# Four GpSimd subtractions of 256 columns for each weight tile's low half, in place of one of 1024

## The chip, the cores and the metric

The kernel runs on one core of a Trainium2 chip. Its time is the device time of one launch in microseconds (us). Of the kernel before there are three runs: 1603.31, 1604.33 and 1604.15 us, median 1604.15 us. A profile of one further execution gives the rows that are read here.

## What is computed

Two layers of a decoder trunk on an input of 512 positions by 1024 channels, float32. Each layer, shortened:

```python
h = rms_norm(x, attn_norm[i])
proj = h @ w_in[i]                      # 1024 x 5376: q, k, v of mixers A, B, C and three gates
ya = moba_attention(...)                # A: blocks of 256, causal
yb = sliding_window_sink_attention(...) # B: window 128, grouped queries, sinks
yc = differential_attention(...)        # C: softmax 1 - lam * softmax 2, then a norm
g = jax.nn.sigmoid(gates)
x = x + (g0 * (ya @ w_pa) + g1 * (yb @ w_pb) + g2 * (yc @ w_pc)) @ w_out[i]
h = rms_norm(x, mlp_norm[i])
u = causal_depthwise_conv(h @ w_up[i], conv_w[i], conv_b[i])
x = x + (silu(gate_u) * val_u) @ w_down[i]
```

## The kernel before

Every product with a weight matrix is computed from two halves of each operand. A weight tile (128 partitions by 1024 columns, `raw`) comes from memory by a transfer on SyncE's queue. ScalarE rounds it to a shorter format (`whi`), and the difference `raw - whi` is the low half (`wlo`). The activations have two halves in the same way (`h0..`, `h1..`, both shown as `h`; those of later products lie in buffers called `slot`). A product is three matmuls into PSUM (`d`): high by high, high by low, low by high. There are 248 weight tiles.

`w_prep` (line 634) makes the two halves of a tile. Line 643 ff. decide which engine subtracts: GpSimd (POOL in the profile) while attention threads are alive and its planned clock is not more than `POOL_LEAD` = 3 us past TensorE's, VectorE (DVE) otherwise. `pump` calls it up to three or four tiles ahead of TensorE; there are 4 buffers each for `whi` and `wlo` and 2 for `raw`, so the transfer of the next tile but one waits until the subtraction has read `raw`.

The order of all instructions is fixed while the program is built. `dense()` emits the weight products block by block. Attention (scores `s`, transposes and products with values `tp`, softmax on ScalarE and VectorE) runs as further threads, and the loop at the end of `trunk` lets a thread emit its next step when a table of planned clocks says that its engine and inputs are ready. That table is `Estimate`: each emitted instruction goes through `Clocked` (line 157; its call in line 168 is why all rows of the profile say L168), and `Estimate.cost` adds its planned duration to the engine's clock, for GpSimd `0.1 + 2.16e-3 * columns` (us). The planned clocks decide the order alone; on the chip the instructions wait for semaphores.

In softmax VectorE runs short chains for each head: the row maximum of the masked scores (`s<-s,mfull`, `mx`), its scaled negative (`nb`), after ScalarE's exponential the reciprocal (`rec`, for mixer C times lambda: `rl`), and scaled probabilities (`slot<-slot,rec`). Rotary embedding is made of products and sums of buffers (`temp`, `slot`). Scores and transposes lie in PSUM, the others in SBUF. GpSimd also computes powers (`rr`, `rsub`, `rn`) and small products (`slot<-slot,vecs`).

Of the kernel before, what the change touches and what calls it, by code (L numbers as in the profile page):

```python
# [11 lines left out]
F32 = mybir.dt.float32  # L12
# [142 lines left out]


class Clocked:
    """Runs an engine's instructions and keeps an estimate of when each one ends."""

    def __init__(self, est, eng, key):  # L160
        self._est, self._eng, self._key = est, eng, key
# [164 lines left out]
def trunk(ctx: ExitStack, tc: tile.TileContext, out: bass.AP, a: dict):  # L326
# [169 lines left out]
    def first_part(t, j):  # L496
        sl = slice(t * 128, (t + 1) * 128)
        ps = tps.get()
        for c in range(4):
            nc.tensor.transpose(ps[:, c, :], X[t][:, (4 * j + c) * 128:(4 * j + c + 1) * 128], identf)  # L500
        for c in range(4):
            k = 4 * j + c
            nc.scalar.activation(H[0, k][:, sl], ps[:, c, :], AF.Copy, scale=gain(0, k))
        for c in range(0, 4, 2):
            nc.scalar.copy(XT[2 * j + c // 2].rearrange("p (e t) -> p e t", e=2)[:, :, sl], ps[:, c:c + 2, :])
        for c in range(4):
            k = 4 * j + c
            nc.vector.scalar_tensor_tensor(H[1, k][:, sl], ps[:, c, :], gain(0, k), H[0, k][:, sl].bitcast(F32),
                                           op0=OP.mult, op1=OP.subtract)
        tps.put(ps)  # L510
# [123 lines left out]
    def w_prep(j):  # L634
        hi = est.alloc("whi", NW, wpool.tile([128, 1024], F32R, tag="whi", name="whi"))
        lo = est.alloc("wlo", NW, wpool.tile([128, 1024], F32R, tag="wlo", name="wlo"))
        raw = RAW.pop(j)
        nc.scalar.copy(hi, raw)
        if state["busy"]:
            t = est.ready(hi)  # L640
            pool = max(est.clock["POOL"], t) <= max(est.clock["DVE"], t) + POOL_BIAS
        else:
            pool = threads[1:] and est.clock["POOL"] <= est.clock["PE"] + POOL_LEAD
        if pool:
            nc.gpsimd.tensor_sub(lo, raw, hi.bitcast(F32))
        else:
            nc.vector.tensor_sub(lo, raw, hi.bitcast(F32))
        if j in wide:
            slots.put(raw)
        if j < 2:  # L650
            first_part(0, j)
        W[j] = (hi, lo)

    def pump(lead):
        while state["prep"] < min(state["fin"] + NW, lead, len(wt)):
            while state["dma"] < min(state["prep"] + ahead(), len(wt)):
                w_dma(state["dma"])
                state["dma"] += 1
            w_prep(state["prep"])
            state["prep"] += 1  # L660
        while state["dma"] < min(state["prep"] + ahead(), len(wt)):
            w_dma(state["dma"])
            state["dma"] += 1
# [888 lines left out]
    def eng_clock(eng):  # L1552
        if eng == "ANY":
            return min(est.clock["ACT"], est.clock["DVE"])
        return est.clock[eng]
# [6 lines left out]
    while threads:  # L1562
# [24 lines left out]
        for r, th in others:  # L1587
            c = eng_clock(th.cur[0])
# [62 lines left out]
```

## Time and profile before

| | |
|---|---|
| median of three runs | 1604.15 us (1603.31 to 1604.33) |
| span of the profiled execution (first to last instruction) | 1599.4 us |
| what the median has beside such a span | 4.75 us |
| TensorE busy | 1546.0 us (97%) |
| VectorE busy | 1077.5 us (67%) |
| ScalarE busy | 789.8 us (49%) |
| GpSimd busy | 293.6 us (18%), 175.5 us of it in 72 subtractions |

The page gives the span of the profiled execution and not its whole device time, so the span stands beside the median here. Shares are means over the whole program: attention of the first layer lies at about 55 to 365 us, that of the second at about 812 to 1160 us; around them are long stretches of weight products alone. The end of a matmul is modelled in the profile: the next one starts 0.23 us after one of 512 columns whose row says 0.39 us, so gaps of TensorE are shown too short by some 0.16 us each.

### The profile page before, as it was taken

The page shows a single profiled execution, that of the slowest core. Times are in us where ns is not written, and L with a number is a line of the kernel's source. Part 1 is how long each engine was busy: PE and PEld are TensorE (multiplying, and loading weights), DVE is VectorE, ACT ScalarE, POOL GpSimd, SP SyncE. Part 2 cuts the span into 40 slices and gives each one's busy share as a digit, 9 for nine tenths or more (in the row PEclk, how much of TensorE's full clock was granted, in tenths as well). Part 3 has the DMA queues.
Part 4 walks back from the last instruction along what each step waited for, and adds up shares of the span by engine and source line. Part 5 has one row for each costly group of instructions (what it writes and reads, how often), then busy time and mean ns, then how long its engine had stood idle before and what let it go on. Part 6 is the DMA issues. An engine that isn't in the chain of part 4 may idle for free.

```text
span 1599.4 us, 21003 instructions
## 1 busy us (share of the span) xinstructions
PE 1546.0 (97%) x7584; PEld 1283.9 (80%) x7584; DVE 1077.5 (67%) x2242; ACT 789.8 (49%) x1534; POOL 293.6 (18%) x243
## 2 busy tenths in 40 slices
PE   8999999999999999999998999999999999999999
PEld 6777787778878888888887887878788788888887
DVE  5998888988576655543269898797875856665321
ACT  7565656755344444333155666647634544443220
POOL 3443343321010000000044553323200100000000
PEclk9999999999999999999999999999999999999999
DMA  5423152223233233333332224322242233223331
GB/s 176 150 57 90 54 198 67 68 65 132 86 100 100 86 105 106 106 99 125 92 113 66 80 67 158 93 80 64 69 151 87 79 106 93 89 83 106 118 119 53
DMA packets 115495, 157.21 MB, mean 98 GB/s; under 512 B 18880, under 2 KB 71104, under 8 KB 115392
## 3 DMA queue, kind: packets, MB, share of 16 engines
q1 hardware_dynamic: 102768, 153.19, 30.6%
q10 hardware_dynamic: 12624, 2.69, 0.8%
q8 instruction: 60, 0.98, 0.2%
q14 instruction: 43, 0.35, 0.1%
HBM read 144.84 MB, written 11.01 MB: 97 GB/s over the span
## 4 chain that ended last, share of the span: by engine, by line
PE 73%; DVE 20%; ACT 3%; issue 2%; POOL 1%; DMA 0%; ACTq 0%; SPq 0%; DVEq 0%; POOLq 0%
PE d L168 67%; DVE slot L168 8%; PE tp L168 5%; DVE temp L168 4%; DVE s L168 2%; ACT slot L168 2%; DVE nb L168 2%; PE s L168 1%; DVE rl L168 1%; DVE wlo L168 1%; DVE h L168 1%; POOL rr L168 1%; ACT whi L168 1%; ACT temp L168 0%; DMA raw<-in_w_in 0%
## 5 line engine op out<-in xcount | busy, mean ns | idle before, releaser
L168 PE MATMUL d<-h,whi 128*128 128x512 f32 x2176 | 683.0, 395 | 8.6 <-DVE h L168 4.5
L168 PEld LDWEIGHTS d<-h,whi 128*128 128x128 f32 x2176 | 399.9, 189 | 88.5 <-DVE h L168 5.6
L168 PE MATMUL d<-h,wlo 128*128 128x512 f32 x1088 | 425.9, 391 | 0.0
L168 DVE TENSOR_TENSOR wlo<-raw,whi 128x1024 fp32r<-128x1024 f32 x174 | 211.1, 1225 | 263.3 <-ACT whi L168 263.1
L168 ACT CAST whi<-raw 128x1024 fp32r<-128x1024 f32 x246 | 256.1, 1051 | 267.1 <-PE d L168 131.8
L168 PE MATMUL d<-slot,whi 128*128 128x512 f32 x864 | 266.6, 390 | 0.0
L168 POOL TENSOR_TENSOR wlo<-raw,whi 128x1024 fp32r<-128x1024 f32 x72 | 175.5, 2438 | 407.9 <-ACT whi L168 368.0
L168 PEld LDWEIGHTS d<-h,wlo 128*128 128x128 f32 x1088 | 204.9, 188 | 44.0 <-DVE wlo L168 0.2
L168 PE MATMUL d<-whi,h 128*128 128x512 f32 (+1 forms) x768 | 207.4, 344 | 0.4 <-ACT h L168 0.4
L168 PEld LDWEIGHTS d<-slot,whi 128*128 128x128 f32 x864 | 161.6, 188 | 33.3
L168 DVE SCALAR_TENSOR_TENSOR temp<-d,packed,temp 128x511 f32<-128x511 f32 (+1 forms) x176 | 127.8, 747 | 68.3 <-ACT temp L168 65.1
L168 PE MATMUL d<-slot,wlo 128*128 128x512 f32 x432 | 168.2, 389 | 0.0
L168 PEld LDWEIGHTS d<-whi,h 128*128 128x128 f32 x768 | 134.5, 191 | 15.5 <-ACT h L168 0.8
L168 ACT CAST slot<-tp 128x256 fp32r<-128x256 f32 (+3 forms) x289 | 102.4, 377 | 83.5 <-PE tp L168 81.0
L168 PE MATMUL d<-wlo,h 128*128 128x256 f32 (+1 forms) x384 | 130.3, 339 | 0.2 <-DVE wlo L168 0.2
L168 ACT ACTIVATE temp<-d,packed 128x512 f32<-128x512 f32 x88 | 67.8, 772 | 92.8 <-PE d L168 85.1
L168 PE MATMUL d<-whi,slot 128*128 128x512 f32 x352 | 108.4, 389 | 0.0
L168 DVE TENSOR_TENSOR slot<-slot,d 128x512 f32<-128x512 f32 x80 | 54.3, 684 | 71.8 <-PE d L168 68.3
L168 PEld LDWEIGHTS d<-slot,wlo 128*128 128x128 f32 x432 | 81.1, 188 | 16.8
L168 ACT CAST slot<-temp 128x256 fp32r<-128x256 f32 (+2 forms) x140 | 58.1, 455 | 65.8 <-DVE temp L168 65.7
L168 POOL TENSOR_TENSOR rn<-nvs,mhalf 128x4 f32<-128x4 f32 x3 | 3.0, 1007 | 475.8 <-DVE nvs L168 475.8
L168 DVE TENSOR_TENSOR slot<-tp,slot 64x128 fp32r<-64x128 f32 (+4 forms) x180 | 75.8, 425 | 18.7 <-ACT slot L168 16.6
(113 smaller groups left out, 1816.6 us busy)
## 6 DMA issues: line engine op xcount, KB each, us to landing
raw<-in_w_up SPq DMA_DIRECT2D x176, 256.0 KB, 3.2
raw<-in_w_in SPq DMA_DIRECT2D x82, 512.0 KB, 3.7
raw<-in_w_down SPq DMA_DIRECT2D x44, 512.0 KB, 3.7
raw<-in_w_out SPq DMA_DIRECT2D x16, 512.0 KB, 4.4
x_spill<-slot SPq DMA_DIRECT2D x8, 512.0 KB, 4.0
b_parked<-slot SPq DMA_DIRECT2D x8, 512.0 KB, 5.1
slot<-b_parked SPq DMA_DIRECT2D x8, 512.0 KB, 7.1
raw<-in_w_pb SPq DMA_DIRECT2D x8, 512.0 KB, 3.7
```

The lines of the kernel that those rows point to most:

```text
L168: r = f(*args, **kw)
```

## The change

In `w_prep` GpSimd's one subtraction over 1024 columns becomes a loop of four over 256 columns each. A line of text in `Clocked` becomes an empty line.

```diff
 class Clocked:
-    """Runs an engine's instructions and keeps an estimate of when each one ends."""
+
...
         if pool:
-            nc.gpsimd.tensor_sub(lo, raw, hi.bitcast(F32))
+            for c in range(0, 1024, 256):
+                nc.gpsimd.tensor_sub(lo[:, c:c + 256], raw[:, c:c + 256], hi[:, c:c + 256].bitcast(F32))
         else:
             nc.vector.tensor_sub(lo, raw, hi.bitcast(F32))
```

The four instructions go through `Estimate` as well, which plans 4 * (0.1 + 2.16e-3 * 256) = 2.61 us for a tile where it planned 0.1 + 2.16e-3 * 1024 = 2.31 us. So later choices of the loop come out otherwise in two stretches (TensorE's instructions that ran at 141 to 365 us and at 926 to 1160 us before); outside them the order is the same. GpSimd makes 70 tiles in 280 instructions where it made 72 in 72; VectorE makes the two others.

TensorE, first layer, the first place where its order differs (at 141 us before). `s_23` and `s_24` are scores of one mixer, `d` the weight product that they are laid between, `tp_41` a sum over a score buffer; numbers in names are running numbers. Before:

```order
L168 MATMUL s_23_1728<-slot_46_940,slot_44_938 128x256
L168 MATMUL d<-h_115,whi 128x512
L168 MATMUL d<-h_123,whi 128x512
L168 MATMUL d<-h_115,wlo 128x512
L168 MATMUL d<-h_116,whi 128x512
L168 MATMUL d<-h_124,whi 128x512
L168 MATMUL d<-h_116,wlo 128x512
L168 MATMUL s_24_1745<-slot_46_940,slot_44_938 128x256
L168 MATMUL tp_41_1752<-onesr,slot_81_1699 128x2 x8
```

And in the changed kernel:

```order
L168 MATMUL s_23_1756<-slot_46_949,slot_44_947 128x256
L168 MATMUL d<-h_115,whi 128x512
L168 MATMUL d<-h_123,whi 128x512
L168 MATMUL d<-h_115,wlo 128x512
L168 MATMUL s_24_1770<-slot_46_949,slot_44_947 128x256
L168 MATMUL d<-h_116,whi 128x512
L168 MATMUL d<-h_124,whi 128x512
L168 MATMUL d<-h_116,wlo 128x512
```

The second score stands three weight matmuls earlier, and the sum `tp_41` later.

GpSimd, first layer, around the powers for mixer B (at 194 to 209 us before). Before:

```order
L168 TENSOR_TENSOR rsub<-vs,mhalf 128x8
L168 COPY slot_83_1777<-rsub 128x512
L168 TENSOR_TENSOR rr<-vv,mhalf 128x8
L168 TENSOR_SCALAR rqB<-rr 128x8
L168 TENSOR_SCALAR nrqB<-rr 128x8
L168 TENSOR_TENSOR rr<-vv,mhalf 128x8
L168 TENSOR_SCALAR rqB<-rr 128x8
L168 TENSOR_SCALAR nrqB<-rr 128x8
L168 TENSOR_TENSOR rr<-vv,mhalf 128x8
L168 TENSOR_SCALAR rqB<-rr 128x8
L168 TENSOR_SCALAR nrqB<-rr 128x8
L168 TENSOR_TENSOR wlo<-raw,whi 128x1024
```

And in the changed kernel:

```order
L168 TENSOR_TENSOR rr<-vv,mhalf 128x8
L168 TENSOR_SCALAR rqB<-rr 128x8
L168 TENSOR_SCALAR nrqB<-rr 128x8
L168 TENSOR_TENSOR rr<-vv,mhalf 128x8
L168 TENSOR_SCALAR rqB<-rr 128x8
L168 TENSOR_SCALAR nrqB<-rr 128x8
L168 TENSOR_TENSOR rr<-vv,mhalf 128x8
L168 TENSOR_SCALAR rqB<-rr 128x8
L168 TENSOR_SCALAR nrqB<-rr 128x8
L168 TENSOR_TENSOR rsub<-vs,mhalf 128x8
L168 COPY slot_83_1797<-rsub 128x512
L168 TENSOR_TENSOR rr<-vv,mhalf 128x2
```

The power for mixer C's norm (`rsub`) and its copy went behind three groups for mixer B, and the subtraction that followed is one of the two that VectorE now makes.

## Rows read from the trace of the kernel before

**Rows 1.** Page, part 1: span, and each engine's busy us, share, instructions.

```profile
span 1599.4 us, 21003 instructions
PE 1546.0 (97%) x7584; PEld 1283.9 (80%) x7584; DVE 1077.5 (67%) x2242; ACT 789.8 (49%) x1534; POOL 293.6 (18%) x243
```

**Rows 2.** Busy us by stretch; columns as in the first line.

```profile
core 0: us, PE busy (x) PEld busy (x) DVE busy (x) ACT busy (x) POOL busy (x), PEclk, DMA share, GB/s
55.00:365.00 310.00, 296.14 (x1630) 246.03 (x1630) 267.57 (x766) 195.07 (x488) 112.64 (x88) 1.00 0.28 87
475.00:812.00 337.00, 336.56 (x1489) 278.44 (x1488) 173.99 (x210) 126.98 (x159) 3.40 (x2) 1.00 0.34 106
812.00:860.00 48.00, 43.98 (x243) 38.26 (x242) 33.75 (x57) 22.16 (x40) 26.89 (x26) 0.93 0.30 87
860.00:1160.00 300.00, 284.09 (x1580) 238.19 (x1580) 253.01 (x727) 194.68 (x484) 114.14 (x88) 1.00 0.28 85
```

**Rows 3.** Tile wlo on GpSimd: durations in ns, and who waited for it.

```profile
L168 POOL TENSOR_TENSOR wlo<-raw,whi x72: 2372/2402/2927, 59.0 to 1267.6; 128x1024 fp32r<-128x1024 f32 x72
...
  PEld tp L168: 1.2, 1
```

**Rows 4.** VectorE's and GpSimd's instructions in time, 266 us: start, us, operation.

```profile
266.50 0.14 DVE L168 DVE_READ_ACCUMULATOR2_ANT mx<- 128x1 f32 x1
266.68 2.31 DVE L168 TENSOR_TENSOR nb<-mx,nrqB 128x2 f32<-128x2 f32 x1
269.02 0.16 DVE L168 TENSOR_TENSOR nb<-nb,nsinks 128x2 f32<-128x2 f32 x1
...
266.56 2.41 POOL L168 TENSOR_TENSOR wlo<-raw,whi 128x1024 fp32r<-128x1024 f32 x1 [7.16 <-ACT whi L168]
```

**Rows 5.** VectorE, first and last instruction held up by a subtraction.

```profile
59.26 2.37 DVE L168 TENSOR_TENSOR temp<-temp,rkC 128x128 f32<-128x128 f32 x1
...
1268.06 2.47 DVE L168 TENSOR_TENSOR h<-slot,h 128x512 fp32r<-128x512 f32 x1 [1.24 <-ACT h L168]
```

**Rows 6.** The chain that ended last, 269 to 284 us: start, us, what.

```profile
266.68 2.32 DVE nb L168
...
270.23 0.34 DVE slot L168
270.58 0.14 issue
270.71 0.51 PE tp L168 x4
```

**Rows 7.** TensorE, first and last gap behind such an instruction.

```profile
68.03 0.68 PE L168 MATMUL tp<-identr,slot 128*128 128x128 f32 x5 [0.50 <-DVE slot L168]
...
1265.67 0.50 PE L168 MATMUL d<-h,whi 128*128 128x512 f32 x1 [0.91 <-DVE h L168]
```

**Rows 8.** GpSimd, seven products of 128 columns without a gap.

```profile
231.98 2.98 POOL L168 TENSOR_TENSOR slot<-slot,vecs 128x128 f32<-128x128 f32 x7 [0.16 <-DMA slot<-in_c_cs]
```

**Rows 9.** GpSimd and VectorE in time, 841 to 852 us.

```profile
841.56 5.05 POOL L168 TENSOR_TENSOR slot<-slot,vecs 128x64 f32<-128x64 f32 x8
842.86 3.01 DVE L168 TENSOR_TENSOR h<-slot,h 128x512 fp32r<-128x512 f32 x4
846.57 2.58 POOL L168 TENSOR_TENSOR wlo<-raw,whi 128x1024 fp32r<-128x1024 f32 x1
846.81 4.86 DVE L168 TENSOR_TENSOR temp<-slot,slot 128x128 f32<-128x128 f32 x2
849.11 2.41 POOL L168 TENSOR_TENSOR wlo<-raw,whi 128x1024 fp32r<-128x1024 f32 x1
```

**Rows 10.** VectorE's own subtractions of a tile, all: busy us, mean ns.

```profile
L168 DVE TENSOR_TENSOR wlo<-raw,whi 128x1024 fp32r<-128x1024 f32 x174 | 211.1, 1225 | 263.3 <-ACT whi L168 263.1
```

**Rows 11.** The GpSimd tile with the least slack, and TensorE's first use of it.

```profile
470.94 2.58 POOL L168 TENSOR_TENSOR wlo<-raw,whi 128x1024 fp32r<-128x1024 f32 x1 [23.48 <-ACT whi L168]
...
476.20 0.40 PE L168 MATMUL d<-h,wlo 128*128 128x512 f32 x1
```

## The prediction

> **What bounds the kernel now.** I read the page's totals first [rows 1]: TensorE is busy for 1546.0 of 1599.4 us, so a change can win only where it stands still or matmuls come late. The table by stretch [rows 2] says where: between the layers (475 to 812 us) TensorE is busy for 336.56 of 337 us, while in attention it misses 310 - 296.14 = 13.86 us in the first layer and 48 - 43.98 + 300 - 284.09 = 19.93 us in the second. There VectorE is the next busiest with 267.57 of 310 us (86%) and 253.01 of 300 us (84%), GpSimd has 36 to 38%.
>
> The tile view of `wlo` [rows 3] seems to say that the subtraction on GpSimd does not matter: 72 tiles of 2.40 us, and one weight load in the whole program waited for them, 1.2 us. The rows in time say otherwise [rows 4]. At 266.56 GpSimd starts a tile; at 266.68 VectorE starts `nb<-mx,nrqB`, two columns, which takes 2.31 us, and the same kind of instruction right behind it takes 0.16 us. The long one ends at 268.99, GpSimd's at 268.97. VectorE is not slowed, it stands until GpSimd's instruction is over. Comparing every VectorE instruction with the others of its operation and shape, I count 60 that end with a GpSimd subtraction in this way, the first at 59.26, the last at 1268.06 [rows 5], together 104.8 us too long. All have two inputs in SBUF, or are a scaling by a scalar within SBUF; instructions that read PSUM (masked maximum, casts of `tp`) are not held. In attention over half of VectorE's instructions are of the held kind (408 of 765 in the first layer, 432 of 784 in the second, counted in the trace). The chain of waits shows what that does [rows 6]: `nb` 2.32 us, the exponential's consumers, then `tp` on TensorE, late.
>
> To price it I follow every start of a matmul that is over 60 ns late (against the usual distance to the one before of its shape) back to what released it. 37 of these gaps have a held VectorE instruction behind them, the first before 68.03, the last before 1265.67 [rows 7], 35.7 us together (14.6 in the first attention, 19.5 in the second, 1.6 at the two norms). That is the sum that this change can touch; about 28 us of gaps in attention have other causes.
>
> **The change part by part.** *The pieces themselves.* GpSimd does seven products of 128 columns in 2.98 us [rows 8], 0.42 each; 1024 columns take 2.40. So a column costs (2.40 - 0.42) / 896 = 2.2 ns, and a piece of 256 columns 0.42 + 128 * 2.2 ns = 0.70 us: a tile takes 2.80 us, 0.40 more, over 70 tiles 28 us. These lie in GpSimd's idle time (it is busy for a third of attention), and nobody waits there: from a tile's end to TensorE's first use I find 7.1 us or more in attention, and the least at all is 476.20 - 473.52 = 2.68 us, at the first norm [rows 11]. Even four held pieces do not use up 7 us. TensorE's extra waits for the parts of a tile are met long before. Cost 0, and if the cover were gone at the two norms, at most 2 us.
>
> *What VectorE gains.* Held instructions now wait for the end of a piece, not of a tile, provided that GpSimd lets one through between two pieces. It does so between two of its instructions, whatever they are [rows 9]: two tiles stand back to back (846.57 and 849.11), and two VectorE products begin at 846.81 and together take 4.86 us, one ending behind each tile. Beside eight short GpSimd products the same engine's four `h<-slot,h` go through one by one, 0.75 us each, while GpSimd's eight take 5.05 us: they alternate. So the first held instruction waits at most one piece's share of the port. I take 0.55 us for that (a quarter of 2.2 us, the usual hold).
>
> But an instruction of the held kind that follows meets the next piece. I walked through the VectorE instructions behind each of the 60, letting one piece go ahead of each that wants SBUF twice, and the pieces run on beside those that do not. At 284 us (`nb`, then four that read PSUM) 2.15 us become 0.50; at 266.68 (two `nb`, then maxima in PSUM) 2.15 become 1.18; at 59.26 (rotary: four held ones in a row) 2.08 stay 2.08, only spread. The sum over the 60 falls from 104.8 to 65.4 us, by 38%. For the 35.7 us on TensorE the bounds are: nothing, if all held instructions come in rows of four; 35.3 us, if each gap is shortened by what the first held instruction behind it wins. I take the proportion of the walk, 35.7 * 0.38 = 13.4 us won, as what is late next is VectorE's own queue, which stays over 75% busy.
>
> *What moves.* The planner puts 0.30 us more on GpSimd's clock for a tile, so two tiles go to VectorE: 2 * 1.225 us [rows 10], and at the rate at which VectorE's held time reaches TensorE (35.7 / 104.8 = 0.34) that is 0.8 us lost. `rsub` and its copy stand behind three power groups on GpSimd; its consumer is a norm before a projection that comes much later, cost 0. The reshuffle on TensorE's queue (scores some matmuls earlier or later between 141 and 365 us and between 926 and 1160 us) no row prices. Over all, attention's matmuls stand 5.7 weight matmuls earlier in the second layer and about as before in the first (counted in the two orders). Its bounds are half of TensorE's idle time there, 33.8 / 2 = 17 us, either way; I take 0, since nothing in the trace favours a side. The transfers on SyncE's queue that wait for a tile's `raw` buffer start 0.4 us later or a little more, against 7 us and more of slack.
>
> *Sum.* -13.4 + 0.8 = -12.6 us on a span of 1599.4, 1586.8 us. The median of the runs is 4.75 us above that span, so 1604.15 - 12.6 = 1591.5 us.
>
> A rule that speaks against the change: the Trainium skill, GPSIMD Engine Reference, section Instruction dispatch, says that each of GpSimd's cores starts the next instruction as soon as its own share of the last is done, with nothing holding them together; SBUF — State Buffer, section SBUF: two separate sides, calls the port pair that VectorE and GpSimd share an exclusive lock for a whole instruction, with deep queues that are not drained to share it. If a row of queued pieces kept the lock on that account, the second rival would follow; VectorE comes through between two queued tiles [rows 9], which speaks against it.
>
> **The rivals.**
> *The wait is only spread.* If held instructions nearly always come four or more in a row, as in rotary at 59.26, the 104.8 us stay and only the two tiles' 0.8 us remain: 1605 us. For it: over half of VectorE's instructions are of that kind. Against: softmax chains, where `nb` and `rl` are held most often, have one or two and then PSUM work.
> *The pieces keep the port.* If VectorE does not come through between queued pieces, each hold grows by 0.40 us: 60 * 0.40 * 0.34 = 8.2 us, with the 0.8 us 1613 us. Against: the two tiles back to back [rows 9].
> *The new order loses.* In the second attention scores and transposes stand 5.7 matmuls, 5.7 * 0.23 = 1.3 us, earlier on TensorE's queue, and where their input is late TensorE now waits that much longer: with the 17 gaps that stand behind held instructions there 22 us, against 12.6 won: 1613.5 us. It decides as soon as more than 10 of the 17 places wait 1.3 us longer. For it: TensorE runs in order and VectorE is 84% busy there. Against: VectorE's results come earlier as well, by 0.5 to 1.6 us.
> *More is won.* If TensorE wins what the first held instruction wins, 1604.15 - 35.3 + 0.8 = 1569.7 us. For it: results go to ScalarE and TensorE head by head, and the first is what they wait for. Against: VectorE's queue.
>
> **How the numbers follow.** The forecast, 1580 to 1600 us, has a chance of 0.62; more won (under 1580) 0.12; only spread 0.12; the new order 0.09; pieces keep the port 0.05. A measurement of this kernel tells about 0.2% from no change, 3.2 us. Faster: 0.60 of the forecast, 0.12, and 0.03 of the spread case, 0.75. Within 0.2%: 0.02, 0.08 and 0.02 of the new order, 0.12. Slower: 0.05, 0.07 and 0.01, 0.13. The range that leaves out some 0.2: down to 1575 us, half of the way into the largest gain, up to 1607 us, which takes in the spread case and leaves out the two at 1613.
>
> **What would show it.** VectorE's busy time in attention falls by some 40 us of 521; `nb` and `rl` have no row over 1 us; GpSimd's pieces have a mean of 0.7 us or more, a tile 2.8 to 4 us from first to last. From 55 to 135 us and from 812 to 920 us the order is unchanged, so what TensorE wins there is the pieces alone; what it wins or loses later has the order in it. I am wrong if VectorE's rows beside pieces still end with the fourth, if TensorE waits for `wlo` in attention, or if its gaps there stay at 62 us.

## The result and the profile after

The changed kernel takes 1585.75 us (median of 4 runs, 1585.06 to 1586.23) against 1603.73 us (1603.26 to 1604.33): 0.9889 of the time, with an interval of 0.9875 to 0.9903, or 18.0 us won. 1591.5 us was forecast. The sign, the place and the mechanism of the forecast hold. Two sizes in it do not: the pieces alone win 23.5 us instead of 13.4, and the new order, with the two tiles that it moves to VectorE, costs about 4.6 us (2.7 to 6.4 by the interval) where 0.8 were taken.

The page of the changed kernel, part 1, answers to [rows 1]:

```profile
span 1584.2 us, 21236 instructions
PE 1543.8 (97%) x7584; PEld 1282.8 (81%) x7584; DVE 1047.2 (66%) x2239; ACT 792.8 (50%) x1539; POOL 338.4 (21%) x451
```

The span is 15.2 us shorter, TensorE's own work hardly changes (1546.0 to 1543.8), VectorE is busy for 30.3 us less although it subtracts for two tiles more, and GpSimd for 44.8 us more. So matmuls come earlier; none became cheaper. The planner's new clocks also exchange some scalings and casts between VectorE and ScalarE: ScalarE runs 1539 instructions instead of 1534, VectorE 2239 instead of 2242 with its two tiles more. Where the new order is spoken of below, this is part of it.

By stretch, with the columns of [rows 2] (the attentions end some us sooner, and the windows with them):

```profile
55.00:361.00 306.00, 295.62 (x1631) 246.14 (x1630) 256.18 (x757) 196.78 (x494) 131.86 (x180) 1.00 0.29 88
474.00:811.00 337.00, 337.00 (x1490) 278.57 (x1490) 173.13 (x206) 127.86 (x159) 3.84 (x5) 1.00 0.34 106
811.00:860.00 49.00, 44.63 (x248) 38.83 (x247) 34.36 (x66) 23.94 (x45) 30.79 (x34) 0.93 0.29 81
860.00:1145.00 285.00, 279.97 (x1566) 235.79 (x1565) 235.31 (x727) 193.16 (x480) 132.46 (x183) 1.00 0.30 89
```

TensorE's idle time goes from 13.86 to 306 - 295.62 = 10.38 us in the first attention and from 15.91 to 285 - 279.97 = 5.03 us in the second. Nothing is won at 811 to 860 us, where rotary's products stand, and the stretch between the layers is as it was. The second layer gives back three times what the first does; the order experiments below say why.

The subtractions on GpSimd (durations in ns, and who waited for a tile) answer to [rows 3] (the last count is of a sample):

```profile
L168 POOL TENSOR_TENSOR wlo<-raw,whi x280: 718/744/1722, 58.9 to 1257.0; 128x256 fp32r<-128x256 f32 x140
...
who waited for it (us, times):
```

The list of those who waited is empty. What the pieces do to VectorE is seen by groups of instructions (busy us, mean ns), first of the kernel before, then of the changed one:

```profile
L168 DVE TENSOR_TENSOR rl<-rec,lam 128x1 f32<-128x1 f32 x32 | 17.6, 551 | 1.1
L168 DVE TENSOR_TENSOR nb<-mx,nrqB 128x2 f32<-128x2 f32 x32 | 11.6, 361 | 1.1
```

```profile
L168 DVE TENSOR_TENSOR rl<-rec,lam 128x1 f32<-128x1 f32 x32 | 7.8, 242 | 1.1
L168 DVE TENSOR_TENSOR nb<-mx,nrqB 128x2 f32<-128x2 f32 x32 | 7.8, 245 | 1.1
```

These instructions take 0.16 us when nothing holds them, so what a mean has above that is hold. Before, 8 of the 32 `rl` took more than 0.2 us, up to 2.36 us; after, 9 did, up to 0.70 us: as many are held, each for less. Counted as for [rows 5], 154 instructions are held for 70.8 us, none by more than 0.61 us, where 60 were held for 104.8 us, by up to 2.23 us.

Where many held instructions stand in a row, next to nothing goes away. VectorE and GpSimd in time at rotary, against [rows 9]:

```profile
843.37 2.02 DVE L168 TENSOR_TENSOR temp<-slot,slot 128x256 f32<-128x256 f32 x3 [1.90 <-POOL slot L168]
845.43 0.84 DVE L168 TENSOR_TENSOR temp<-temp,temp 128x256 f32<-128x256 f32 x1
846.31 0.71 DVE L168 TENSOR_TENSOR temp<-temp,rkC 128x128 f32<-128x128 f32 x1
846.94 2.41 DVE L168 TENSOR_TENSOR temp<-slot,slot 128x256 f32<-128x256 f32 x3
...
843.58 6.35 POOL L168 TENSOR_TENSOR wlo<-raw,whi 128x256 fp32r<-128x256 f32 x8
```

Eight pieces in one block on GpSimd, and VectorE's eight products beside them, about one per piece. The two engines take turns instruction by instruction. The Trainium skill, SBUF — State Buffer, section SBUF: two separate sides, describes the pair of ports that the two share as a lock that one instruction keeps to its end; this agrees with the traces (a hold is never longer than one piece), and the row shows in addition that the lock changes hands between two queued pieces, which was what the change needed.

### The profile page after: what moved, and what is told of

It is laid out like the page before. It is cut to its first block, busy times and chain, and to the rows that moved or that the text cites. A ratio compares the mean times of both kernels' runs of the same rounds, so it can differ in the third digit from the quotient of the medians.

```text
span 1584.2 us, 21236 instructions
## 1 busy us (share of the span) xinstructions
PE 1543.8 (97%) x7584; PEld 1282.8 (81%) x7584; DVE 1047.2 (66%) x2239; ACT 792.8 (50%) x1539; POOL 338.4 (21%) x451
## 4 chain that ended last, share of the span: by engine, by line
PE 78%; DVE 16%; ACT 3%; issue 1%; POOL 1%; DMA 1%; SPq 0%; DVEq 0%; ACTq 0%; POOLq 0%
PE d L168 71%; DVE slot L168 6%; PE tp L168 6%; DVE temp L168 4%; DVE s L168 2%; PE s L168 1%; ACT slot L168 1%; DVE nb L168 1%; ACT whi L168 1%; DVE h L168 1%; DVE wlo L168 1%; POOL rr L168 0%; ACT h L168 0%; ACT L168 0%; DVE rl L168 0%
## 5 line engine op out<-in xcount | busy, mean ns | idle before, releaser
L168 DVE TENSOR_TENSOR wlo<-raw,whi 128x1024 fp32r<-128x1024 f32 x176 | 214.9, 1233 | 272.4 <-ACT whi L168 269.4
L168 POOL TENSOR_TENSOR wlo<-raw,whi 128x256 fp32r<-128x256 f32 x280 | 218.3, 812 | 359.8 <-ACT whi L168 347.1
L168 ACT CAST slot<-temp 128x256 fp32r<-128x256 f32 (+2 forms) x140 | 58.5, 456 | 65.4 <-DVE temp L168 65.2
```

Of the source, the lines that this page charges most:

```text
L168: r = f(*args, **kw)
```

## The experiments

Each is one edit of the kernel before, run beside it on the same chip. In this kernel an engine wrapped by the planner (`nc`) also advances the planner's estimate; `core` below is the same engine without it, and `est.note` advances the estimate alone. So what runs and what the planner believes can be set apart. Ratios are to the kernel before, with the interval. "Late" is the sum over all matmuls of how much later each starts than its shape's usual distance after the one before, however small (37.7 us of it lie at the 37 places of [rows 7], where 35.7 us were counted above a threshold of 60 ns). It accounts for the spans: before to changed 15.0 us less late, 15.2 us less span. "Held" counts an instruction whose excess over its usual time is clear of the scatter.

| what runs | order of | ratio | span, us | held on VectorE: times, us | late on TensorE, us: all / at the 37 places / elsewhere |
|---|---|---|---|---|---|
| before, 1 x 1024 | before | 1 | 1599.4 | 60, 104.8 | 75.7 / 37.7 / 37.9 |
| 2 x 512 | before | 0.992 (0.9907 to 0.9934) | 1586.5 | 101, 87.5 | 63.0 / 25.8 / 37.1 |
| 4 x 256 | before | 0.9853 (0.984 to 0.9867) | 1575.0 | 148, 65.0 | 51.6 / 14.5 / 37.1 |
| 8 x 128 | before | 0.9798 (0.9784 to 0.9811) | 1565.2 | 197, 46.6 | 42.1 / 3.9 / 38.2 |
| 16 x 64 | before | 0.9794 (0.9781 to 0.9807) | 1567.5 | at least 151, 24.4 | 44.5 / 1.4 / 43.1 |
| 32 x 32 | before | 1.0166 (1.0152 to 1.0179) | 1621.2 | at least 39, 7.0 | 98.1 |
| nothing read | before | 0.9723 (0.9709 to 0.9736) | 1554.2 | 5, 3.2 | 31.3 / 0.0 / 31.2 |
| 1 x 1024 | changed | 1.0029 (1.0017 to 1.004) | 1604.2 | 56, 97.5 | 80.2 |
| changed, 4 x 256 | changed | 0.9889 (0.9875 to 0.9903) | 1584.2 | 154, 70.8 | 60.7 |

With 64 and 32 columns many holds are of some 0.1 us and less, and the count leaves such ones out. VectorE's busy time on the pages does not depend on a count: from 1024 down to 32 columns in the order of before it is 1077.5, 1060.1, 1040.2, 1024.4, 1016.3 and 1012.3 us, and 978.2 us where nothing is read.

**The pieces without the new order.**

```
-            nc.gpsimd.tensor_sub(lo, raw, hi.bitcast(F32))
+            for c in range(0, 1024, 256):
+                core.gpsimd.tensor_sub(lo[:, c:c + 256], raw[:, c:c + 256], hi[:, c:c + 256].bitcast(F32))
+            est.note("POOL", "tensor_sub", (lo, raw, hi.bitcast(F32)), {})
```

> Four pieces of 256 columns, but the planner is told of one subtraction of 1024, so every engine has exactly the order of the kernel before and GpSimd keeps its 72 tiles. Theory (shorter holds of VectorE make the gain): 1586 to 1592 us, most of the 18 us. Rival (the new order made the gain): 1600 us or more. Held time of VectorE by both about 70 us in place of 104.8.

Measured: 1576.8 against 1600.61 us, 0.9853, 23.5 us by the ratio: clearly more than the changed kernel wins, and more than was expected here. TensorE's late starts fall by 23.2 us at the 37 places and by 0.8 us everywhere else. The walk's forecast of held time was 65.4 us; 65.0 were measured. So the sum of the holds came out as worked out, and what TensorE makes of them did not. The place of [rows 4] and [rows 6] shows how. VectorE before, behind the rows of [rows 4], then VectorE and GpSimd in this kernel:

```profile
269.88 0.16 DVE L168 TENSOR_TENSOR nb<-mx,nrqB 128x2 f32<-128x2 f32 x1
...
270.15 0.62 DVE L168 TENSOR_TENSOR slot<-temp,slot 128x256 fp32r<-128x256 f32 x2
```

```profile
261.98 0.62 DVE L168 TENSOR_TENSOR nb<-mx,nrqB 128x2 f32<-128x2 f32 x1
262.63 0.66 DVE L168 TENSOR_TENSOR nb<-nb,nsinks 128x2 f32<-128x2 f32 x1
...
263.99 0.69 DVE L168 TENSOR_TENSOR nb<-mx,nrqB 128x2 f32<-128x2 f32 x1
...
261.84 2.83 POOL L646 TENSOR_TENSOR wlo<-raw,whi 128x256 fp32r<-128x256 f32 x4 [5.61 <-ACT whi L168]
```

And TensorE's transposes behind them, before and then with the pieces (in brackets the idle time ahead):

```profile
270.71 0.51 PE L168 MATMUL tp<-identr,slot 128*128 128x128 f32 x4 [1.13 <-DVE slot L168]
```

```profile
265.36 0.51 PE L168 MATMUL tp<-identr,slot 128*128 128x128 f32 x4 [0.49 <-DVE slot L168]
```

The transposes wait for the product of rotary (`slot<-temp,slot`) that stands a few instructions behind the `nb` on VectorE. Before, one `nb` is held for 2.15 us. Here three are, the third by the last piece: 0.46 + 0.50 + 0.53 = 1.49 us (the walk had 1.18 for this place). TensorE's idle time falls from 1.13 to 0.49 us; with the 0.16 us by which the profile shows such gaps too short, the transposes start 1.29 us late before and 0.65 us late here. Both times that is about 0.85 us less than the hold. The same place with 512 and then with 128 columns:

```profile
265.16 1.21 DVE L168 TENSOR_TENSOR nb<-mx,nrqB 128x2 f32<-128x2 f32 x1
266.40 1.21 DVE L168 TENSOR_TENSOR nb<-nb,nsinks 128x2 f32<-128x2 f32 x1
...
269.14 0.51 PE L168 MATMUL tp<-identr,slot 128*128 128x128 f32 x4 [1.07 <-DVE slot L168]
```

```profile
257.94 0.34 DVE L168 TENSOR_TENSOR nb<-mx,nrqB 128x2 f32<-128x2 f32 x1
258.31 0.38 DVE L168 TENSOR_TENSOR nb<-nb,nsinks 128x2 f32<-128x2 f32 x1
...
259.59 0.37 DVE L168 TENSOR_TENSOR nb<-nb,nsinks 128x2 f32<-128x2 f32 x1
...
260.68 0.45 PE L168 MATMUL tp<-identr,slot 128*128 128x128 f32 x4
```

Two pieces of 512 columns hold 1.04 + 1.05 = 2.09 us and the transposes are 1.23 us late, 0.86 us less; 128 columns hold 0.18 + 0.22 + 0.21 = 0.61 us, and they are not late. So at this place VectorE's result has a lead of some 0.86 us on TensorE, and only the part of the holds beyond that reaches it: above the lead every us taken off a hold counts in full, below it none does. That was worked out for this place alone. At the 13 of the 37 places where the walk left over 80% of the held time, the lateness still fell by about half, from some 12 to 6 us, and to under 3 with 128 columns; at the other 24 from some 26 to 8 and 1.

**The new order without the pieces.**

```
-            nc.gpsimd.tensor_sub(lo, raw, hi.bitcast(F32))
+            core.gpsimd.tensor_sub(lo, raw, hi.bitcast(F32))
+            for c in range(0, 1024, 256):
+                est.note("POOL", "tensor_sub", (lo[:, c:c + 256], raw[:, c:c + 256], hi[:, c:c + 256].bitcast(F32)), {})
```

> One subtraction of 1024 columns, but the planner is told of four of 256, so every engine has the order of the changed kernel and VectorE makes the two tiles. Theory: 1601 to 1607 us, since holds are as long as before. Rival (the new order made the gain): 1586 to 1592 us.

Measured: 1604.57 us, 1.0029: 4.6 us lost, though fewer instructions are held (56, 97.5 us), and within the range expected of unchanged holds. 0.9853 * 1.0029 = 0.9882, and the changed kernel has 0.9889: the two parts add up. It lies in the first layer: TensorE's 1872nd matmul, at the end of the first attention, starts at 365.4 us before and 371.0 here; with pieces at 355.3 in the old order, 361.3 in the new.

One place where the new order loses, in this kernel (VectorE, GpSimd, TensorE in time):

```profile
352.64 3.34 DVE L168 TENSOR_SCALAR slot<-slot,rec 128x256 f32<-128x256 f32 x4
...
352.64 2.39 POOL L645 TENSOR_TENSOR wlo<-raw,whi 128x1024 fp32r<-128x1024 f32 x1 [2.90 <-ACT whi L168]
...
356.72 0.63 PE L168 MATMUL tp<-identf,slot 128*128 128x128 f32 x4 [1.39 <-DVE slot L168]
```

And the same instructions in the changed kernel:

```profile
343.77 3.12 DVE L168 TENSOR_SCALAR slot<-slot,rec 128x256 f32<-128x256 f32 x4
...
343.78 2.97 POOL L168 TENSOR_TENSOR wlo<-raw,whi 128x256 fp32r<-128x256 f32 x4 [2.50 <-ACT whi L168]
...
347.64 0.63 PE L168 MATMUL tp<-identf,slot 128*128 128x128 f32 x4 [1.19 <-DVE slot L168]
```

In this order a tile falls together with four scalings in a row ahead of a transpose, and pieces hardly help (1.39 to 1.19 us); with pieces in the old order there is no such gap. With pieces in the old order the first attention leaves 4.48 us of TensorE's time idle, where the changed kernel leaves 10.38:

```profile
55.00:355.00 300.00, 295.52 (x1632) 247.23 (x1632) 251.50 (x766) 194.87 (x488) 134.87 (x184) 0.99 0.28 90
```

The instance shown is worth 1.2 to 1.4 us; the other 3 us were not followed to single instructions.

**The new order in the second layer alone.** The edit is the first one, with four notes for tiles of the second layer and one for those of the first:

```
+                if j >= 124:
+                    est.note("POOL", "tensor_sub", (lo[:, c:c + 256], raw[:, c:c + 256], hi[:, c:c + 256].bitcast(F32)), {})
+            if j < 124:
+                est.note("POOL", "tensor_sub", (lo, raw, hi.bitcast(F32)), {})
```

> Four pieces of 256; the planner is told of one subtraction in the first layer and of four in the second, so TensorE's order is that of before in the first layer and that of the changed kernel in the second. If the new order's loss lies in the first layer, where attention ends 6 us later than with the old order: 0.985 to 0.9875 of before. If it lies in the second layer: 0.988 to 0.990.

Measured: 1578.35 against 1601.68 us, 0.9852 (0.9839 to 0.9865), the same as with the old order throughout (0.9853); the intervals leave room for some 2 us. In the stretch of the second layer where the order differs, TensorE is late by 11.3 us here and in the changed kernel and by 10.1 us in the old order with pieces; in that of the first layer by 9.9 us in the old order with pieces and by 16.2 us in the changed kernel, and without pieces by 19.0 and 23.3 us. So nearly all of the loss is in the first layer. (GpSimd makes 71 tiles here, one less than before and one more than in the changed kernel.)

**GpSimd reads nothing.**

```
-            nc.gpsimd.tensor_sub(lo, raw, hi.bitcast(F32))
+            core.gpsimd.memset(lo.bitcast(F32), 0.0)
+            est.note("POOL", "tensor_sub", (lo, raw, hi.bitcast(F32)), {})
```

> Order of before; GpSimd fills the low half of its 72 tiles with zeros in place of subtracting (the output leaves those low halves out), so that it writes SBUF and reads nothing of it. Theory: VectorE's instructions with two inputs in SBUF are hardly held, held time under 20 us; this is the most that any split can give: 1568 to 1580 us. Rival (holds do not matter for the end): 1600 us or more. If the hold is on the write side, held time stays some 50 us or more.

Measured: 1556.25 us, 0.9723. Page and tile view of this kernel:

```profile
span 1554.2 us, 20923 instructions
PE 1533.9 (99%) x7584; PEld 1284.1 (83%) x7584; DVE 978.2 (63%) x2242; ACT 787.9 (51%) x1534; POOL 186.8 (12%) x243
...
L645 POOL MEMSET wlo<- x72: 942/954/998, 50.8 to 1214.9; 128x1024 f32 x72
```

No product, sum or difference of two SBUF inputs is held by a fill, VectorE is busy for 99.3 us less, and all lateness at the 37 places is gone; the gain is above the range expected. That shows the holds as the cause, beyond the match of end times: GpSimd still writes 1024 columns of the same tiles at the same points of the order. The same section of the Trainium skill says that an instruction of VectorE with two inputs in SBUF stands back only for one of GpSimd that reads SBUF; the trace agrees (54 instructions of the kinds that were held start within a fill with a quarter of a us or more of it left, and none stands for it, but for one that queues behind the scaling shown next). Scalings by a scalar within SBUF are another matter: none of the seven that start within a fill gets through before its end, and five of them stand 0.28 to 0.78 us too long, 3.2 us together. The first of the five, which takes 0.28 us when free:

```profile
172.78 0.98 DVE L168 TENSOR_SCALAR slot<-slot,rec 128x128 f32<-128x128 f32 x1
...
172.73 0.95 POOL L645 MEMSET wlo<- 128x1024 f32 x1 [10.70 <-PE d L168]
```

So a fill, which reads nothing, still holds scalings; what held the instructions with two SBUF inputs was that the subtraction reads. The 2.8% are a bound for what cutting the subtraction can win, and a generous one: 37.9 - 31.2 = 6.7 us of the lateness that went away lay outside the 37 places, where shorter holds win nothing (37.1 with 256 columns). A fill of 0.95 us also frees GpSimd sooner, and `raw` is not read by it; either may be the reason, which was not tested.

**Other sizes.** The edit is the first one, with 512, 128, 64 or 32 columns in place of 256.

> Order of before, two pieces of 512 columns. Theory (what decides is how far one hold exceeds the time by which VectorE's result is ahead of TensorE): held time some 85 us, a hold at most 1.1 us, and 0.8 to 1.2% faster than before, more than half of what four pieces win. Rival (gain in proportion to held time, at 0.34): 0.3 to 0.5%.

> Order of before, eight pieces of 128 columns for a tile. Theory: the first hold is half as long again, but a tile occupies GpSimd for 3.4 us or more and meets more instructions: 1584 to 1592 us, within 3 us of the four pieces. Rival (a held instruction's cost is per piece, not per column): slower than four pieces by 5 us or more.

> Order of before, 16 pieces of 64 columns for a tile. A tile takes 4.5 us or more on GpSimd. Theory (the length of one hold decides, and GpSimd has slack): held time falls to about 30 us, 0.2 to 0.5% faster than eight pieces on the same chip. Rival (the number of holds decides, or GpSimd's tiles come late): as fast as eight pieces or slower.

> Order of before, 32 pieces of 32 columns for a tile, some 7 us on GpSimd without VectorE's share, about the least slack that tiles have in attention. Theory: no faster than 16 pieces, since tiles now come late for TensorE or transfers; the gain of shorter holds is spent. Rival (only the hold's length counts): faster again, near the kernel whose GpSimd reads nothing, 0.972 of before.

Measured: the table. Per us of held time that is taken away, the time falls by 12.8 / 17.3 = 0.74 us for 512 columns (0.61 to 0.86 by the ratio's interval), 23.5 / 39.8 = 0.59 for 256 (0.53 to 0.64) and 32.3 / 58.2 = 0.56 for 128 (time from the ratio on 1600.6 us). Each is well above the 0.34 that the average hold was worth, and the first cut, which takes off the longest holds, may be worth the most. Of the expectations, that for 512 columns holds at its lower end (0.8%), that for 128 misses (1584 us or more was expected, 1567.32 measured), that for 64 misses (its rival, as fast as eight pieces, holds), and that for 32 holds. From 128 to 64 columns VectorE's busy time falls by another 8.1 us and nothing is won: the lateness falls from 3.9 to 1.4 us at the 37 places and rises from 38.2 to 43.1 us elsewhere. At the norms a tile of 64-column pieces takes up to 7.9 us, and at the first norm TensorE waits for one:

```profile
461.71 0.50 PE L168 MATMUL d<-h,wlo 128*128 128x512 f32 x1 [0.87 <-POOL wlo L646]
```

With 32 columns GpSimd is the bound. First attention by stretch, the chain of waits there, and two of the program's waits (us, times, longest):

```profile
55.00:365.00 310.00, 295.17 (x1619) 247.98 (x1618) 238.75 (x765) 194.04 (x486) 279.72 (x1061) 0.98 0.27 85
```

```profile
by line: POOL wlo L646 29.7%; PE d L168 28.9%; PE tp L168 8.6%; DVE slot L168 6.0%; DMA raw<-in_w_in 4.8%; POOL rr L168 4.3%; PE s L168 3.6%; ACT slot L168 3.1%; ACT whi L168 1.7%; issue 1.6%; DVE temp L168 1.5%; DVE s L168 1.5%; DVE nb L16
```

```profile
ACT whi L168 <- DMA raw<-in_w_in: 47.1, 21, 5.7
...
DVE vv L168 <- POOL rr L168: 16.2, 6, 5.6
```

GpSimd is busy for 279.72 of 310 us, and its holds are short (VectorE is busy for 34.1 us more than where nothing is read, 99.3 us before). But tiles end late, so `raw` buffers come free late and ScalarE waits 47.1 us for their loads (4.8 us before), and VectorE waits for the powers that stand behind the pieces in GpSimd's queue. The cover that the forecast named for the pieces' extra time is real, and this is what stands behind it.

**One kind of instruction freed.** 96 one-column `nb` and the 32 `rl` become a scaling by a scalar; the subtraction is left at 1024 columns, and the planner is told of the instruction before. `mx_` and `sc_` are the maximum and its factor; the branch for more than one column, which stays as it was, is left out.

```
+                core.vector.tensor_scalar(nb, mx_, sc_, None, op0=OP.mult)
+                est.note("DVE", "tensor_mul", (nb, mx_, sc_), {})
...
-                nc.vector.tensor_mul(rl, rec[:, 1:2], lam[:, l:l + 1])
+                core.vector.tensor_scalar(rl, rec[:, 1:2], lam[:, l:l + 1], None, op0=OP.mult)
+                est.note("DVE", "tensor_mul", (rl, rec[:, 1:2], lam[:, l:l + 1]), {})
```

> Order of before and one subtraction of 1024 columns; the 96 one-column products nb of mixers A and C and the 32 products rl are scalings by a scalar in place of products of two tensors. If a scaling of one column is not held by GpSimd, held time falls by some 25 to 30 us (the short softmax steps are 45 of the 104.8 us) and, if these short steps are what TensorE waits for, the time by 0.7 to 1.1%. Rival (all holds count alike, at 0.34 of their length): 0.5% or less. If a scaling of one column is held too, nothing changes: within 0.2% of before.

Measured: 1599.68 us, 0.9989 (0.998 to 0.9998), 58 holds of 96.0 us: one column is not held, and yet held time falls by 8.8 us and not by 25 or more, and next to nothing is won. VectorE and GpSimd in time, before and then here:

```profile
107.34 1.77 DVE L168 TENSOR_TENSOR rl<-rec,lam 128x1 f32<-128x1 f32 x1
109.15 0.42 DVE L168 TENSOR_SCALAR slot<-slot,rl 128x384 f32<-128x384 f32 x1
```

```profile
108.08 0.21 DVE L1114 TENSOR_SCALAR rl<-rec,lam 128x1 f32<-128x1 f32 x1
108.33 1.68 DVE L168 TENSOR_SCALAR slot<-slot,rl 128x384 f32<-128x384 f32 x1
...
107.40 2.39 POOL L168 TENSOR_TENSOR wlo<-raw,whi 128x1024 fp32r<-128x1024 f32 x1 [4.05 <-ACT whi L168]
```

`rl` is no longer held, and the scaling right behind it is, to the same end. Here the hold passes to the next instruction that can be held; that this is so at the other places, too, was not followed. The 128 scalings also take 0.05 us longer each than the products did, 7 us together.

**The version to keep** is 8 x 128 with the order of before: 1567.32 us, 0.9798 of the time before where the changed kernel has 0.9889, with 46.6 us held and the two attentions at 292.31 of 295 and 319.71 of 323 us of TensorE (its own windows); 16 x 64 is as fast. By stretch with 128 columns:

```profile
55.00:350.00 295.00, 292.31 (x1633) 246.61 (x1632) 245.21 (x766) 194.81 (x488) 156.27 (x312) 1.00 0.28 90
801.00:1124.00 323.00, 319.71 (x1810) 272.76 (x1809) 258.81 (x783) 215.74 (x520) 184.62 (x352) 1.00 0.28 90
```

## Why the prediction was right, and where it was not

*What is held, and by what: right.* Without GpSimd's reads no product of two SBUF inputs is held any more, only five scalings by fills; with pieces of 256 columns no hold is over 0.61 us, and a piece takes 0.72 us or more.

*How a hold gets to TensorE: the place right, the path not.* The prediction read [rows 6] as `nb`, the exponential's consumers, then `tp`. No exponential is in that chain: behind the held `nb` stand VectorE's next instructions in their order, and the transposes wait for the product of rotary among them (270.15, above). So a hold reaches TensorE through whatever stands behind it on VectorE, not only through softmax.

*That GpSimd lets VectorE through between pieces: right*, read from two tiles in [rows 9], and the walk built on it gave 65.4 us of held time for 65.0 measured (in the old order; 70.8 in the changed kernel). That the sum is so close is in part luck: at 266.68 us it had 1.18 for 1.49.

*"I take the proportion of the walk, 35.7 * 0.38 = 13.4 us won": the step that failed.* The same pieces were worth 23.2 of 37.7 us on TensorE at the same places, 62%, for 38% of the held time. A late matmul is the hold less the lead that VectorE's result had, and the proportion takes the lead for zero. With a lead, each us taken off a hold that outlasts it counts in full. At 270.71 us that lead could have been read from the trace before: a hold of 2.15 us and an idle time of 1.13 us [rows 4, 6], 1.29 with the 0.16 that the profile hides, leave 0.86 us, and the same lead gives the lateness with 512, 256 and 128 columns. For the other 36 places it is an argument that fits their sums. Of holds in a row, the first consumer sees only those ahead of its own input, so a row may cost TensorE less than its sum. The condition of the lower bound, "nothing, if all held instructions come in rows of four", was not met: at the 13 places where the walk left most of the held time, about half of the lateness still went. At rotary, where such a row does stand, little did: the first transpose behind it is some 4.2 us late before, 3.7 with 256 columns and 1.9 with 128.

*"The reshuffle: I take 0": wrong by 4.6 us.* It lay within the bounds of 17 us. The rival "the new order loses" had the mechanism roughly and the layer wrong: the second layer, where matmuls were counted to stand 5.7 places earlier, loses a us or two at most, and the first, where they stood on average as before, loses nearly all. An average displacement says little about which few instructions now coincide with a tile. With 0.8 us for the two extra tiles, which were not measured apart and are part of the 4.6, the sum was -13.4 + 0.8; the runs say -23.5 + 4.6, which is 18.9 us won, and the changed kernel itself 18.0. The errors had opposite signs, so it is luck that the time came out closer than its terms.

*GpSimd's cost: right.* Nobody waited for a tile, and 0.40 us more per tile cost nothing at this size. It does with 32 columns, and with 64 at the first norm. At the first norm, where the slack was 2.68 us [rows 11], a tile took 4.88 us (466.85 to 471.73) and TensorE's first use of it came at 471.53, before its last piece was done: the pieces are waited for one by one.

*The signs named.* VectorE's busy time in attention fell from 520.6 to 491.5 us, 29.1 where 40 were said; two more tiles (2.45 us) and the 5.4 us by which the changed kernel is held longer than the walk found (70.8 for 65.4) account for most of the rest. No `nb` or `rl` is held by over 0.61 us. A tile takes 2.8 to 3.8 us but for that one and one of 4.27. In 55 to 135 us, where the order is unchanged, TensorE is busy for 78.27 us where it was 76.67, and in 812 to 920 us for 103.01 where it was 100.42: that is the pieces alone. At rotary the wait behind the products is not shorter (4.37 us, before 4.02), as the walk had it.

Still open: whether the lead accounts for the other 36 places one by one, which moved instructions of the first layer cost the rest of the 4.6 us, and whether an order planned for 128 columns would do better than the one of before.

## What to carry to other kernels

When two engines exclude each other by instruction, price what a hold has beyond the consumer's lead, not a share of the sum of held time: cutting the blocking instruction in a few pieces can win more than the sum says. Stop before the pieces' fixed part makes the blocking engine late (here at 128 columns; 64 wins no more, 32 loses). When a planner sees the edit, run the edit and the new order apart: each had a sign of its own here.

## What was not expected of the hardware

A short instruction of GpSimd costs more than its columns: a tile's pieces follow one another at about 0.70 us for 256 columns (four in 2.83 us), against 2.40 us for 1024 in one. With 32 columns GpSimd's time over the program is 680.5 us, where it was 293.6.

A scaling by a scalar at one column is not held at all (`rl`, 214 ns mean over 32 instructions; of the 128 freed, 16 start within a tile and none takes over 0.22 us), while the same operation over 384 columns is (1.68 us beside a tile), and a product of two tensors of one column is too (1.77 us).

A fill of 128x1024 on GpSimd, which reads nothing, takes 0.95 us and holds no product of two SBUF inputs; a scaling by a scalar within SBUF it does hold (0.98 us where it takes 0.28).
